# Single-pass matrix products that read their columns from two halves in turn, in a two-layer encoder kernel

## The chip, the cores and the metric

The kernel runs on one core of one Trainium2 chip. The metric is the device time of one execution in microseconds (us), the median of the runs. Kernels that are compared ran on the same chip.

## The reference

The model has two layers on 512 frames of width 1024 and 256 memory tokens. Everything is float32. Layer 0 mixes time with a gated recurrence (12 heads of 64), layer 1 with chunked attention; both also attend to the memory, project the result back and add a gated feed-forward block with a short convolution:

```python
p = rms_norm(x, ln1) @ w_in               # 1024 -> mixer columns | memory queries
mix = rwkv7_time_mix(...)                 # layer 0;  chunk_attention(...) in layer 1
mo = memory_attention(q_mem, mem_n, w_mem_kv[layer])
x = x + jnp.concatenate([mix, mo], -1) @ w_out[layer]
gate, val = jnp.split(rms_norm(x, ln2) @ ffn_in, 2, -1)      # 1024 -> 2 x 2816
conv = conv_b + sum(conv_w[j] * shifted(gate, 2 - j) for j in range(3))
x = x + (gelu(conv, approximate=False) * val) @ ffn_out      # 2816 -> 1024
```

## The kernel before

Activations lie with features on the 128 partitions and the 512 frames along the free dimension. Every large product is done in two parts of float32r ("single-pass" here, against plain float32): a tile is split into a high part (a rounded copy, by ScalarE) and a low part (the rest, by VectorE, or by a DMA that adds into it), and three matmuls per tile of the contraction, high x high, high x low and low x high, are summed in PSUM. A matmul has a stationary operand of 128 columns, loaded ahead of it (PEld in the profile), and a moving operand whose columns are streamed through the array.

The places that the change and the prediction's steps touch:

- `dense` (L233 to L248) makes one 128 x 512 product from 8 tiles of the contraction with 24 matmuls. The weights `whi`, `wlo` are stationary and the 512 frames of the activations (`r1h`, `r1l`, `r2h`, `r2l`) move. It serves the projections of both mixers, `out_proj` (L396) and, with 256 memory tokens, `mem_kv` (L1040).
- `ffn` (L415 to L929) has three parts. First the `mixer` generator prepares operands while `out_proj` runs. Then come 21 frames per layer, one for each 128 of the 2816 hidden columns (the last tile goes through `dense`). A frame (`Seven.frame`, L537) makes gate and value with seven products in place of eight, each of 128 x 256 columns from 4 tiles, by `prod` (L427): 12 matmuls, 84 for the frame. Their results stand in the PSUM tiles `f1` to `f4`, read by one ScalarE copy (L553) and five VectorE sums (L509, L572, L585, L601, L603). Inside a frame the instructions of VectorE and ScalarE are pinned in the order in which they are written (`keep`). VectorE also makes the sums of weights for the next frame and the low parts (L486, L491, L495, L504, L481); three DMAs of POOL's queue add into tiles (`wlv` L471, `wlo` L477, `tmp` L522). Every second frame (`APART`) leaves half of one low part to such a DMA.
- Last, `out_by_seven` (L763) projects back. There the hidden activations are stationary and the weights move, 512 columns at a time (`rows`, L692 to L703), again with seven products for eight (L749 and after).
- `v_proj` (L1754) and the values of `mem_kv` (L1055 to L1062) also have the weights as moving operand, 256 columns at a time. The scores of the attention (L1788, L1789) and the score of the memory attention move 128 to 512 columns of keys; transposes, small products of the recurrence and the products with the attention weights (L370, L1817) are in plain float32.

The program is one straight list per engine, and the order is set when it is built: by the order in which the code is written, by `weave` (L87), which interleaves generators by estimated costs, and by a scheduler that keeps dependencies.

Of the kernel before, what the change touches and what calls it, by code (L numbers as in the profile page):

```python
# [12 lines left out]
AF = mybir.ActivationFunctionType  # L13
# [46 lines left out]
def _constants():  # L60
    f = np.float32
    c = np.zeros((P, NCST), f)

    def put(name, a):
        o, n = COFF[name]
        c[:, o:o + n] = a

    i = np.arange(P)
    same = (i[:, None] // 64) == (i[None, :] // 64)
    put("ident", np.eye(P, dtype=f))  # L70
    put("ones_d", np.full((P, 2), 1.0 / 1024, f))
# [12 lines left out]
    return c  # L84

# [36 lines left out]
def trunk_kernel(ctx, tc, A, out):  # L122
# [97 lines left out]
    def mm3(ps, wh, wl, ah, al, start, stop):  # L220
        PE.matmul(ps, wh, ah, start=start, stop=False)
        PE.matmul(ps, wh, al, start=False, stop=False)
        PE.matmul(ps, wl, ah, start=False, stop=stop)
# [8 lines left out]

    def dense(ps, units, act, order=None, start=True, stop=True):  # L233

        ks = [(w, j, k) for w, kk in units for j, k in enumerate(kk)]
        if order is not None:
            ks = [next(q for q in ks if q[2] == k) for k in order]

        for n, ((wh, wl), j, k) in enumerate(ks):
            ah, al = act(k)  # L240
            PE.matmul(ps, wh[:, j * P:(j + 1) * P], ah, start=start and n == 0, stop=False)  # L241
            dense_at[0] = PE.matmul(ps, wh[:, j * P:(j + 1) * P], al, start=False, stop=False)  # L242
            yield 432
        for n, ((wh, wl), j, k) in enumerate(ks):
            dense_at[0] = PE.matmul(ps, wl[:, j * P:(j + 1) * P], act(k)[0], start=False,  # L245
                                    stop=stop and n == len(ks) - 1)
            if n % 2 or n == len(ks) - 1:
                yield 432 if n % 2 else 216  # L248
# [149 lines left out]
    def out_proj(l, act, taken, xT, order, pre=(), done=()):  # L398
        for m in range(KD):
            if m < len(pre):  # L400
                w, ps = pre[m]
                run(dense(ps[:], [(w, K8)], act, order=[k for k in order if k not in done], start=False))
            else:
                w = load_w(A["w_out"][l, m])
                ps = ps_f() if m in (2, 3) else ps_d()
                run(dense(ps[:], [(w, K8)], act, order=order))
            V.tensor_tensor(xT[:, m], xT[:, m], ps[:], op=ALU.add)
            next(taken)
# [8 lines left out]
    def ffn(l, hp, U, T, new_x, xT, after=None, tokens=None):  # L417
# [7 lines left out]
        XU = lambda o, h: [tuple(t[:, 2 * k + o, h * 256:h * 256 + 256] for t in (Uh, Ul)) for k in range(4)]  # L425
        XT = lambda i: [tuple(t[:, 2 * k + i // 2, i % 2 * 256:i % 2 * 256 + 256] for t in (Th, Tl)) for k in range(4)]
# [20 lines left out]
        class Seven:  # L447
# [59 lines left out]
            def end1(self):  # L507
                g, f4 = self.g, self.f4
                keep(V.tensor_tensor(g[:], g[:], f4[:], op=ALU.add))  # L509
# [24 lines left out]
            def end5(self):  # L534
                keep(V.tensor_tensor(hid32[self.j], self.v[:], self.c[:], op=ALU.mult))

            def frame(self, prev2, prev, nxt, norm=None, ending=None):  # L537
# [15 lines left out]
                keep(SC.copy(g[:, h1], f1[:, h1]))  # L553
# [18 lines left out]
                keep(V.tensor_tensor(g[:, h2], g[:, h1], f2[:, h1], op=ALU.subtract))  # L572
# [12 lines left out]
                keep(V.tensor_tensor(c[:, h1], f1[:, h2], g[:, h2], op=ALU.subtract))  # L585
# [11 lines left out]
                if first:  # L597
# [3 lines left out]
                keep(V.tensor_tensor(v[:].rearrange("p (a s) -> p a s", a=2), c[:, h1].unsqueeze(1).to_broadcast([P, 2, 256]),  # L601
                                     f3[:].rearrange("p (a s) -> p a s", a=2), op=ALU.add))
                keep(V.tensor_tensor(g[:, h2], g[:, h2], f3[:, h2], op=ALU.subtract))  # L603
# [11 lines left out]
        def ending():  # L615
# [30 lines left out]
            keep(V.tensor_tensor(g[:], pg[:], rho[:], op=ALU.mult))  # L646
            run(dense(pv[:], [(wv[:2], KO)], pair_of(Uh, Ul)))
            tile21 = Seven(j)
            tile21.g, tile21.c, tile21.v = g, c, pv
# [42 lines left out]
        def rows(pss, act, k0, ch, first, last):  # L692
            hi, lo, n = ch
            for t, ps in pss:
                ts = slice(t * P, t * P + P)
                for i in range(n):
                    for a in act:
                        PE.matmul(ps[:], a[:, k0 + i, ts], hi[:, i * S:i * S + S],  # L698
                                  start=bool(first) and (first is True or t in first) and a is act[0] and i == 0, stop=False)
            for t, ps in pss:  # L700
                ts = slice(t * P, t * P + P)
                for i in range(n):
                    PE.matmul(ps[:], act[0][:, k0 + i, ts], lo[:, i * S:i * S + S], start=False, stop=bool(last) and t in last and i == n - 1)  # L703
# [311 lines left out]
    def lora_pair(idx, w, wm):  # L1015
# [6 lines left out]
        V.tensor_tensor(b_[:], pb[:], rho[:], op=ALU.mult)  # L1022
        z = tmp()
        V.tensor_tensor(z[:], pa[:], rho[:], op=ALU.mult)
# [14 lines left out]
    def mem_kv():  # L1039
# [3 lines left out]
        for l in range(2):  # L1043
            km, vm_ = (kmT0, vm0) if l == 0 else (tmp(F32, (P, 2, 256)) for _ in range(2))
            for f in range(2):
                w = load_w(A["w_memk"][l, f])
                ps = ps_l()
                yield from dense(ps[:, :NMEM], [(w, K8)], pair_of(mh, ml))
                yield from norm
                V.tensor_tensor(km[:, f], ps[:, :NMEM], macc[:, NMEM:], op=ALU.mult)  # L1050
            ps = [ps_l(), ps_l()]
            for u in range(2):
                wh, wl = load_w(A["w_memv"][l, u])
                for j in range(4):
                    k = u * 4 + j  # L1055
                    for t in range(2):
                        ws = slice(j * 256, (j + 1) * 256)
                        ts = slice(t * P, (t + 1) * P)
                        pt = ps[t][:, :256]
                        PE.matmul(pt, mh[:, k, ts], wh[:, ws], start=k == 0, stop=False)  # L1060
                        PE.matmul(pt, ml[:, k, ts], wh[:, ws], start=False, stop=False)
                        PE.matmul(pt, mh[:, k, ts], wl[:, ws], start=False, stop=k == 7)  # L1062
                    yield 650
# [35 lines left out]
    def head_wide(src, fix, bank, tied=False):  # L1099
# [5 lines left out]
        with behind_dense() if tied else ExitStack():  # L1105
            PE.matmul(ps[:], blk1[:], hi[:], start=True, stop=False)
            PE.matmul(ps[:], blk1[:], lo[:], start=False, stop=True)
        a, y, sh = tmp(), tmp(), tmp()
        fix(a[:], ps[:])
# [16 lines left out]
    def prepare(i, T):  # L1126
# [13 lines left out]
        PE.matmul(pz[:], wah[:, 0], zw[:], start=True, stop=False)  # L1140
        PE.matmul(pa[:], wah[:, 1], zs[:], start=True, stop=False)
        PE.matmul(pz[:], wal[:, 0], zw[:], start=False, stop=True)
        PE.matmul(pa[:], wal[:, 1], zs[:], start=False, stop=True)
# [3 lines left out]
        SC.activation(sig[:], pz[:], AF.Tanh, scale=0.5, bias=aw0h[:, 6 + i:7 + i])  # L1147
        V.tensor_scalar(sig[:], sig[:], 0.5, 0.5, op0=ALU.mult, op1=ALU.add)
        th = kt_("a")
        SC.activation(th[:], pa[:], AF.Tanh, scale=0.5, bias=aw0h[:, i:i + 1])  # L1150

        def proj(j, nm, nxt):
# [7 lines left out]
            V.tensor_tensor(p_[:], ps[:], rho[:], op=ALU.mult)  # L1160
# [99 lines left out]
        def bonus():  # L1260
# [8 lines left out]
            PE.matmul(pb[:], blk1[:], rkh[:], start=True, stop=False)  # L1269
            PE.matmul(pb[:], blk1[:], rkl[:], start=False, stop=True)  # L1270
# [14 lines left out]
        V.tensor_tensor(bon[:], T["pb"][:], T["v"][:], op=ALU.mult)  # L1285
# [218 lines left out]
    def dst_mix(i, yc, pg):  # L1504
        V.tensor_tensor(yc[:], yc[:], pg[:], op=ALU.mult)
# [5 lines left out]
    def q_mem(src, act, qm):  # L1511
        for f in range(2):
# [3 lines left out]
            V.scalar_tensor_tensor(qm[f], ps[:], 0.125, rho[:], op0=ALU.mult, op1=ALU.mult)  # L1516
# [169 lines left out]
    with ExitStack() as bctx:  # L1686
# [38 lines left out]
        def q_split(ps, T):  # L1725
            q = tmp()
            V.scalar_tensor_tensor(q[:], ps[:], 0.125, rho[:], op0=ALU.mult, op1=ALU.mult)
# [7 lines left out]
        def k_proj(i, T, ps=None):  # L1735
# [6 lines left out]
            V.tensor_tensor(k_[:], ps[:], rho[:], op=ALU.mult)  # L1742
# [11 lines left out]
        def v_proj(g, wv=None):  # L1754
# [3 lines left out]
            for t2 in range(2):  # L1758

                pp_ = ps_d() if g else ps_s()  # L1760
                for t in (2 * t2, 2 * t2 + 1):
                    pt = pp_[:, (t % 2) * 256:(t % 2) * 256 + 256]
                    ts = slice(t * P, (t + 1) * P)
                    for k in range(8):
                        wh, wl = wv[k // 4]
                        ws = slice((k % 4) * 256, (k % 4 + 1) * 256)
                        PE.matmul(pt, r1h[:, k, ts], wh[:, ws], start=k == 0, stop=False)
                        PE.matmul(pt, r1l[:, k, ts], wh[:, ws], start=False, stop=False)
                        PE.matmul(pt, r1h[:, k, ts], wl[:, ws], start=False, stop=k == 7)
# [191 lines left out]

def layout(i):
# [26 lines left out]
    A["w_memv"] = np.stack([_vtile(g["w_mem_kv"][l][:, 256:])[0] for l in range(2)])  # L1989
# [13 lines left out]
    A["ffn_out7"] = np.stack(seven)  # L2003
    A["ffn_outp"] = np.stack(plain)
    A["lnf"] = np.ascontiguousarray(np.broadcast_to(g["ln_f"][None, :], (P, KD * P)))
    A["w_kvk"] = _wtile(g["w_kv"][:, :768])
    A["w_kvv"] = _vtile(g["w_kv"][:, 768:])
# [24 lines left out]
```

## Time and profile before

| | |
|---|---|
| runs | 1291.62, 1293.07, 1292.89 us, median 1292.89 |
| span of the profiled execution | 1292.6 us (0.3 us under the median of the runs) |
| mean granted TensorE clock | 0.997 |
| busy: PE, PEld, DVE, ACT, POOL | 98%, 84%, 80%, 65%, 12% |
| DMA | 192.14 MB moved, mean 149 GB/s |

The profile is of one execution. PE rows are matmuls; they are pipelined, so that one begins before the one ahead of it ends, and the step from start to start is what a matmul costs in a stream. A group `psf<-th,whi` writes the PSUM tile `psf` from `th` and `whi`; `128*128 128x256` is the stationary shape, then the output. Idle time is told with what ended it. A window row gives, for a stretch of time, each engine's busy us and number of instructions, the granted clock, the DMA engines' busy share and GB/s.

### The profile page before, as it was taken

To read this page: it belongs to the slowest core of one execution; us is meant where nothing else is said; L and a number is where in the kernel's file an instruction comes from. 1 tells how busy PE (TensorE), PEld (TensorE's weight loads), DVE (VectorE), ACT (ScalarE), POOL (GpSimd) and SP (SyncE) were. 2 spreads that over 40 slices of the span, in tenths; PEclk is the share of its full clock that TensorE was granted. 3 is DMA by queue.
4 is the path that set the end of the run, shared out by engine and by line. 5 is a ranking of instruction groups with operands and counts; after the bars stand their busy time and mean duration, and the time that the engine had idled before them with its cause. 6 is when DMAs were issued, how large, how long until landed. Compare 5 with 4: busy or idle time off the path is not lost.

```text
span 1292.6 us, 26432 instructions
## 1 busy us (share of the span) xinstructions
PE 1260.9 (98%) x10420; PEld 1083.1 (84%) x10420; DVE 1031.7 (80%) x1956; ACT 846.4 (65%) x1398; POOL 152.7 (12%) x182
## 2 busy tenths in 40 slices
PE   9999999999999999999999999999999999999997
PEld 7887777777789999998888878787789999998886
DVE  7867677765688999998876876658889999998684
ACT  6566767856476777776554676757757777765662
POOL 1000000000001222320220000000002222211200
PEclk9999999999999999999999999999999999999999
DMA  5364444453055988996984322234429989978951
GB/s 204 110 174 106 100 96 89 92 109 96 30 166 126 212 198 198 206 208 172 274 185 122 118 87 82 76 104 123 130 61 212 197 193 211 208 161 262 233 149 66
DMA packets 95581, 192.14 MB, mean 149 GB/s; under 512 B 22112, under 2 KB 30432, under 8 KB 95456
## 3 DMA queue, kind: packets, MB, share of 16 engines
q1 hardware_dynamic: 68592, 129.14, 31.9%
q0 software_dynamic: 26864, 61.31, 27.3%
q8 instruction: 82, 1.34, 0.4%
q14 instruction: 43, 0.35, 0.1%
HBM read 174.20 MB, written 6.29 MB: 140 GB/s over the span
## 4 chain that ended last, share of the span: by engine, by line
PE 62%; DVE 15%; ACT 8%; DMA 8%; issue 6%; SPq 0%; POOL 0%; ACTq 0%; DVEq 0%; POOLq 0%
PE psf L434 8%; PE psf L698 7%; PE psd L245 6%; PE psd L241 5%; PE psd L242 5%; DMA wlv<-in_ffn_in_dram 4%; PE psf L436 4%; PE psf L703 4%; PE psd L698 3%; ACT whi L499 2%; DMA wraw<-in_ffn_in_dram 2%; PE psd L703 2%; DVE raw L486 1%; PE pss L1817 1%; DVE wlo L504 1%
## 5 line engine op out<-in xcount | busy, mean ns | idle before, releaser
L499 ACT CAST whi<-raw 128x1024 fp32r<-128x1024 f32 (+1 forms) x168 | 153.3, 942 | 62.3 <-PE psf L434 29.5
L434 PE MATMUL psf<-th,whi 128*128 128x256 f32 x672 | 161.4, 278 | 2.5 <-ACT tmp L553 1.9
L434 PE MATMUL psf<-tl,whi 128*128 128x256 f32 x672 | 161.1, 276 | 0.0
L195 ACT CAST whi<-wraw 128x1024 fp32r<-128x1024 f32 x84 | 87.6, 1048 | 78.3 <-PE psd L242 37.4
L434 PEld LDWEIGHTS psf<-th,whi 128*128 128x128 f32 x672 | 125.8, 188 | 3.9 <-ACT tmp L553 2.9
L434 PEld LDWEIGHTS psf<-tl,whi 128*128 128x128 f32 x672 | 126.0, 188 | 0.0
L504 DVE TENSOR_TENSOR wlo<-raw,whi 128x1024 fp32r<-128x1024 f32 (+1 forms) x108 | 109.3, 1012 | 9.1 <-ACT whi L499 8.9
L241 PE MATMUL psd<-r1h,whi 128*128 128x512 f32 x264 | 107.4, 408 | 0.0
L242 PE MATMUL psd<-r1l,whi 128*128 128x512 f32 x264 | 105.0, 398 | 0.0
L203 DVE TENSOR_TENSOR wlo<-wraw,whi 128x1024 fp32r<-128x1024 f32 x65 | 79.2, 1219 | 22.3 <-ACT whi L195 20.4
L688 ACT CAST whi<-raw 128x1024 fp32r<-128x1024 f32 (+1 forms) x52 | 49.6, 954 | 59.9 <-PE psf L698 33.1
L689 DVE TENSOR_TENSOR wlo<-raw,whi 128x1024 fp32r<-128x1024 f32 (+1 forms) x52 | 56.5, 1097 | 38.9 <-ACT whi L688 31.5
L436 PE MATMUL psf<-th,wlo 128*128 128x256 f32 x504 | 78.0, 276 | 0.0
L245 PE MATMUL psd<-r1h,wlo 128*128 128x512 f32 x264 | 74.3, 403 | 0.6 <-DMA wlo<-in_ffn_in_dram 0.4
L471 POOL DMA_DIRECT2D wlv<-in_ffn_in_dram x40 | 60.7, 1516 | 59.5 <-DVE tmp L572 59.1
L436 PEld LDWEIGHTS psf<-th,wlo 128*128 128x128 f32 x504 | 66.8, 188 | 0.0
L434 PE MATMUL psf<-r2h,whi 128*128 128x256 f32 x252 | 60.9, 278 | 0.7 <-ACT whi L499 0.7
L434 PE MATMUL psf<-r1h,whi 128*128 128x256 f32 x252 | 60.7, 277 | 0.7 <-ACT whi L499 0.7
L434 PE MATMUL psf<-r2l,whi 128*128 128x256 f32 x252 | 60.7, 277 | 0.0
L434 PE MATMUL psf<-r1l,whi 128*128 128x256 f32 x252 | 60.6, 277 | 0.0
L241 PEld LDWEIGHTS psd<-r1h,whi 128*128 128x128 f32 x264 | 49.6, 188 | 12.0 <-issue 2.1
L525 ACT ACTIVATE tmp<-tmp,vec 128x512 f32<-128x512 f32 x44 | 36.0, 817 | 33.3 <-DVE tmp L512 33.3
(611 smaller groups left out, 3576.8 us busy)
## 6 DMA issues: line engine op xcount, KB each, us to landing
raw<-in_ffn_in_dram SPq DMA_DIRECT2D x42, 512.0 KB, 5.2
raw<-in_ffn_in_dram SPq DMA_DIRECT2D x84, 256.0 KB, 5.5
wlv<-in_ffn_in_dram POOLq DMA_DIRECT2D x40, 512.0 KB, 8.6
raw<-in_ffn_out_dram SPq DMA_DIRECT2D x30, 512.0 KB, 6.2
raw<-in_ffn_out_dram POOLq DMA_DIRECT2D x24, 512.0 KB, 8.4
wraw<-in_wA_dram SPq DMA_DIRECT2D x20, 512.0 KB, 4.1
wraw<-in_w_out_dram SPq DMA_DIRECT2D x16, 512.0 KB, 4.1
wraw<-in_ffn_outp_dram SPq DMA_DIRECT2D x16, 512.0 KB, 4.5
```

Source lines behind the costliest of these rows:

```text
L195: high = lambda: pin(SC.copy(hi[:, :n], raw))
L203: pin(V.tensor_tensor(lo[:, :n], raw, hi[:, :n], op=ALU.subtract))
L241: PE.matmul(ps, wh[:, j * P:(j + 1) * P], ah, start=start and n == 0, stop=False)
L242: dense_at[0] = PE.matmul(ps, wh[:, j * P:(j + 1) * P], al, start=False, stop=False)
L245: dense_at[0] = PE.matmul(ps, wl[:, j * P:(j + 1) * P], act(k)[0], start=False, stop=stop and n == len(ks) - 1)
L434: PE.matmul(ps, wh[:, o + k * P:o + k * P + P], x[k][n], start=k == n == 0, stop=False)
L436: PE.matmul(ps, wl[:, ol + k * P:ol + k * P + P], x[k][0], start=False, stop=k == 3)
L471: GP.dma_start(self.low[:].rearrange("p (a s) -> p a s", a=2), self.second, accum_op=ALU.add)
L499: keep(SC.copy(hi[:, :n], self.pair(what) if n > S else self.raw[:, what]))
L504: keep(V.tensor_tensor(lo[:, :n], self.pair(what) if n > S else self.raw[:, what], hi[:, :n], op=ALU.subtract))
L698: PE.matmul(ps[:], a[:, k0 + i, ts], hi[:, i * S:i * S + S], start=bool(first) and (first is True or t in first) and a is act[0] and i == ...
L703: PE.matmul(ps[:], act[0][:, k0 + i, ts], lo[:, i * S:i * S + S], start=False, stop=bool(last) and t in last and i == n - 1)
```

## The change

Wherever a product in float32r has 512 or 256 columns, its moving operand is now read through a view that takes one column from the first half of the range, one from the second half, the next of the first, and so on (`woven`). The matmul writes its output without gaps, so the columns stand in PSUM in that mixed order. Whoever reads them out reads one half of the columns with a step of 2 from PSUM and then the other half with a step of 2 (`plain_order`), and writes the two halves one behind the other (`halved` splits the SBUF side into the same shape). Where the weights move (`rows`, `v_proj`, the values of `mem_kv`) the host stores the weights in the opposite order (`_woven`), so that the output comes out in plain order and the readers stay as they were. Plain float32 products, transposes and the scores of the attention are as before. The diff, cut to its core:

```diff
+def woven(t):
+    return t.rearrange("p (a b) -> p b a", a=2)
+def halved(t):
+    return t.rearrange("p (a b) -> p a b", a=2)
+def plain_order(ps):
+    return ps.rearrange("p (b a) -> p a b", a=2)
...
+    def moving(hl):
+        return [woven(t) for t in hl]
...
     def dense(ps, units, act, order=None, start=True, stop=True):
-            ah, al = act(k)
+            ah, al = moving(act(k))
...
-        XU = lambda o, h: [tuple(t[:, 2 * k + o, h * 256:h * 256 + 256] for t in (Uh, Ul)) for k in range(4)]
+        XU = lambda o, h: [tuple(woven(t[:, 2 * k + o, h * 256:h * 256 + 256]) for t in (Uh, Ul)) for k in range(4)]
...
-                keep(SC.copy(g[:, h1], f1[:, h1]))
+                keep(SC.copy(halved(g[:, h1]), plain_order(f1[:, h1])))
...
-                keep(V.tensor_tensor(g[:, h2], g[:, h1], f2[:, h1], op=ALU.subtract))
+                keep(V.tensor_tensor(halved(g[:, h2]), halved(g[:, h1]), plain_order(f2[:, h1]), op=ALU.subtract))
...
-                        PE.matmul(ps[:], a[:, k0 + i, ts], hi[:, i * S:i * S + S],
+                        PE.matmul(ps[:], a[:, k0 + i, ts], woven(hi[:, i * S:i * S + S]),
...
-            V.tensor_tensor(p_[:], ps[:], rho[:], op=ALU.mult)
+            V.tensor_tensor(halved(p_[:]), plain_order(ps[:]), halved(rho[:]), op=ALU.mult)
...
+def _woven(w, n=S):
+    return np.ascontiguousarray(w.reshape(*w.shape[:-1], -1, n // 2, 2).swapaxes(-1, -2)).reshape(w.shape)
...
-    A["ffn_out7"] = np.stack(seven)
+    A["ffn_out7"] = _woven(np.stack(seven))
```

The readers that got the step are those of `out_proj` (L407), of the frames (L509, L553, L572, L585, L601, L603) and of the last hidden tile (L646, L535), and those of the projections (L1022, L1024, L1050, L1109, L1147, L1150, L1160, L1285, L1505, L1516, L1727, L1742).

No instruction is added, removed or moved: on every engine the same operations stand in the same order. Only some of PE's waits differ: 191 rows of its list wait for an earlier matmul's own count (PE_49) where 165 did. Most of the added ones are in the frames whose first low part VectorE makes. This is PE's list before, at the second product of such a frame (`th`, `tl` are the summed activations, `r2h` a high part, `whi` and `wlo` the weights):

```order
L436 MATMUL psf<-r2h,wlo 128x256 [waits DVE_49]
L436 MATMUL psf<-r2h,wlo 128x256 x3
L434 MATMUL psf<-th,whi 128x256
L434 MATMUL psf<-tl,whi 128x256
L434 MATMUL psf<-th,whi 128x256
```

And this is PE's list at the same place now:

```order
L452 MATMUL psf<-r2h,wlo 128x256 [waits DVE_49]
L452 MATMUL psf<-r2h,wlo 128x256 x3
L450 MATMUL psf<-th,whi 128x256 [waits PE_49]
L450 MATMUL psf<-tl,whi 128x256
L450 MATMUL psf<-th,whi 128x256
```

The matmuls are the same; the first of the second product has got a wait for a matmul that stands ahead of it on the same engine.

More of the change, by code (lines that the diff above doesn't have):

```diff
@@ L220, in mm3 @@
     def mm3(ps, wh, wl, ah, al, start, stop):
+        ah, al = woven(ah), woven(al)
         PE.matmul(ps, wh, ah, start=start, stop=False)
@@ L244, in dense @@
         for n, ((wh, wl), j, k) in enumerate(ks):
-            dense_at[0] = PE.matmul(ps, wl[:, j * P:(j + 1) * P], act(k)[0], start=False,
+            dense_at[0] = PE.matmul(ps, wl[:, j * P:(j + 1) * P], moving(act(k))[0], start=False,
                                     stop=stop and n == len(ks) - 1)
@@ L702, in rows @@
                 for i in range(n):
-                    PE.matmul(ps[:], act[0][:, k0 + i, ts], lo[:, i * S:i * S + S], start=False, stop=bool(last) and t in last and i == n - 1)
+                    PE.matmul(ps[:], act[0][:, k0 + i, ts], woven(lo[:, i * S:i * S + S]), start=False, stop=bool(last) and t in last and i == n - 1)
         def seventh(pss, raw, act, first=True, last=True, read=None, side=()):
@@ L1268, in bonus @@
             pb = ps_s()
-            PE.matmul(pb[:], blk1[:], rkh[:], start=True, stop=False)
-            PE.matmul(pb[:], blk1[:], rkl[:], start=False, stop=True)
+            PE.matmul(pb[:], blk1[:], woven(rkh[:]), start=True, stop=False)
+            PE.matmul(pb[:], blk1[:], woven(rkl[:]), start=False, stop=True)
             T["pb"] = pb
@@ L1766, in v_proj @@
                         ws = slice((k % 4) * 256, (k % 4 + 1) * 256)
[L1767 to L1769 removed]
+                        PE.matmul(pt, r1h[:, k, ts], woven(wh[:, ws]), start=k == 0, stop=False)
+                        PE.matmul(pt, r1l[:, k, ts], woven(wh[:, ws]), start=False, stop=False)
+                        PE.matmul(pt, r1h[:, k, ts], woven(wl[:, ws]), start=False, stop=k == 7)
                         yield 324
```

68 lines of the change are left out of this document (35 added, 33 removed).

## The prediction

> **What bounds the kernel now.** I read the page first: its span, busy times and chain of waits.
>
> ```profile
> span 1292.6 us, 26432 instructions
> PE 1260.9 (98%) x10420; PEld 1083.1 (84%) x10420; DVE 1031.7 (80%) x1956; ACT 846.4 (65%) x1398; POOL 152.7 (12%) x182
> PE 62%; DVE 15%; ACT 8%; DMA 8%; issue 6%; SPq 0%; POOL 0%; ACTq 0%; DVEq 0%; POOLq 0%
> ```
>
> PE is busy nearly throughout and holds 62% of the chain. The shares differ by stage, so next the windows: the frames of layer 0 and of layer 1, the two stretches in which the hidden activations are projected back, the first mixer, the first `out_proj`, and the second mixer with the end of layer 0's projection.
>
> ```profile
> 395.45:590.02 194.57, 192.07 (x1667) 190.29 (x1667) 185.55 (x287) 140.74 (x189) 49.70 (x48) 1.00 0.87 194
> 953.98:1150.95 196.97, 191.96 (x1670) 190.36 (x1670) 186.14 (x287) 142.31 (x189) 49.65 (x48) 1.00 0.87 192
> 600.00:690.00 90.00, 89.30 (x396) 73.28 (x396) 72.13 (x74) 51.50 (x62) 13.88 (x16) 1.00 0.86 227
> 1161.00:1292.60 131.60, 123.67 (x558) 101.31 (x556) 95.08 (x124) 65.61 (x88) 13.87 (x16) 0.99 0.65 180
> 0.00:345.00 345.00, 334.18 (x4321) 259.92 (x4322) 248.82 (x674) 227.07 (x448) 18.33 (x36) 1.00 0.44 110
> 345.00:390.00 45.00, 45.00 (x204) 35.98 (x203) 33.79 (x54) 26.84 (x38) 1.75 (x2) 1.00 0.45 141
> 690.00:950.00 260.00, 255.99 (x1389) 204.66 (x1388) 185.97 (x427) 168.78 (x358) 3.75 (x14) 1.00 0.31 97
> ```
>
> PE is busy for 94% or more of each. Beside it VectorE (the third pair) is busy 95% in the frames, about 80% in the projections back and 72% in the mixers; the DMA engines reach 0.86 or 0.87 in the frames and the first projection back. So PE sets the time almost everywhere, and in the frames VectorE is close behind. The granted clock is full throughout. What one matmul costs PE is its step from start to start, which the timeline gives, here of 512-column, then of 256-column products:
>
> ```profile
> 600.27 0.39 PE L241 MATMUL psd<-r2h,whi 128*128 128x512 f32 x1
> ...
> 601.40 0.39 PE L242 MATMUL psd<-r2l,whi 128*128 128x512 f32 x1
> 1001.48 0.28 PE L434 MATMUL psf<-r1h,whi 128*128 128x256 f32 x1
> ...
> 1002.39 0.28 PE L436 MATMUL psf<-r1h,wlo 128*128 128x256 f32 x1
> ```
>
> Five steps take 1.13 us, 0.226 each; eight take 0.91, 0.114 each. That is 0.442 and 0.444 ns a column: the cost grows with the columns and leaves no room for a fixed part. Products in plain float32 read the same kind of tile:
>
> ```profile
> 334.83 0.59 PE L370 MATMUL pss<-E,vm 128*64 128x512 f32 x1
> 335.25 0.59 PE L370 MATMUL pss<-KB,vm 128*64 128x512 f32 x1
> ```
>
> Each takes 0.42 us for 512 columns. It goes over them at about half the pace, and half of 0.42 is 0.21, not 0.226. So the array can step faster than the single-pass products let it; about 7% of their time by these rounded rows goes with the columns that pass at the full pace. Reading the moving operand is the obvious suspect, and its order is what the change alters.
>
> **Products of 512 columns.** How many there are by stage: the windows of the weights' high parts, which two of each three matmuls use.
>
> ```profile
> 0.00:345.00 345.00, 131.72 (x521) 88.23 (x521) 21.77 (x18) 36.99 (x37) 1.00 0.44 110
> 345.00:390.00 45.00, 30.28 (x129) 23.27 (x127) 7.30 (x6) 7.13 (x7) 1.00 0.45 141
> 600.00:690.00 90.00, 62.94 (x256) 47.72 (x256) 34.13 (x31) 30.00 (x31) 1.00 0.86 227
> 690.00:950.00 260.00, 151.12 (x630) 108.13 (x630) 40.47 (x34) 35.59 (x34) 1.00 0.31 97
> 1161.00:1292.60 131.60, 83.11 (x336) 62.08 (x334) 39.20 (x35) 34.23 (x35) 0.99 0.65 180
> ```
>
> Less the 256-column ones that the code puts there (128 and 192), times 1.5: 590, 194, 384, 657 and 504, together 2329. The price of a woven read does not stand in this trace. From below, at full pace it cannot be under 0.205 us, half of 0.42 with its rounding, a gain of 21 ns; from above it is unbounded, since each read could pay for a change of place (a rival). I take 0.215, half of 0.42 rounded up, since the rows nearest to it pass as many columns: a gain of about 12 ns. That is 7.1, 2.3, 4.6, 7.9 and 6.0 us. The second and third stages hardly have idle PE, and I keep 2.3 and 4.2, the latter for the crowded DMA engines. The mixers hold serial chains of small products, where a faster `dense` only arrives early: I keep three quarters, 5.3 and 5.9. The last stage ends with idle PE, 5.5. Sum 23 us.
>
> The Trainium skill (TensorE: Matmul & The Clock Gate, Back-to-back issue gap) gives for an isolated warm matmul columns / 2.4 + 2.5 ns, 216 ns for 512; the trace does not agree, with 226. By it the gain would be at most about 10 ns a product, 19 us in place of 23.
>
> **Frames.** A frame has 84 matmuls, 84 x 0.1135 = 9.53 us, yet the 20 frames of the first window take 194.57 / 20 = 9.73 us and the second's 9.85. Two things cap what faster reads give. First the weights: a product of only two columns still follows the one ahead of it by
>
> ```profile
> 24.13 0.47 PE L311 MATMUL pss<-cst,acc 128*128 128x2 f32 x3
> L311 PE MATMUL pss<-cst,acc x32: 165/251/272, 23.7 to 954.2; 128*128 128x2 f32 x32
> ```
>
> (0.47 - 0.25) / 2 = 0.11 us, since each loads 128 columns of weights. A 256-column product at 0.1135 can come down to that, not below: up to 3.5 ns, 0.29 us a frame, 12 us for all 42. Second VectorE, whose instructions stand in one pinned row from one low part to the next frame's:
>
> ```profile
> 1110.95 1.22 DVE L504 TENSOR_TENSOR wlo<-raw,whi 128x1024 fp32r<-128x1024 f32 x1
> ...
> 1118.25 1.23 DVE L504 TENSOR_TENSOR wlo<-raw,whi 128x1024 fp32r<-128x1024 f32 x1 [0.31 <-ACT whi L499]
> ...
> 1120.92 1.22 DVE L504 TENSOR_TENSOR wlo<-raw,whi 128x1024 fp32r<-128x1024 f32 x1
> ```
>
> Such a frame takes it 9.97 us with 0.31 idle; the frame between has a shorter low part. So VectorE has hardly any room, and a faster PE will wait for its low parts, or for the late `wlv`:
>
> ```profile
> PE psf L436 <- DMA wlv<-in_ffn_in_dram: 4.1, 7, 1.6
> ```
>
> I take 4 us of the 12, ends 0 and 12. The other 480 products of 256 columns give 1 us. Total 23 + 4 + 1 = 28.
>
> **Readers.** Five sums on VectorE read PSUM in each frame:
>
> ```profile
> L601 DVE TENSOR_TENSOR tmp<-tmp,psf 128x512 f32<-128x512 f32 x42 | 28.6, 680 | 0.2
> L509 DVE TENSOR_TENSOR tmp<-tmp,psf 128x512 f32<-128x512 f32 x42 | 28.5, 679 | 0.0
> L585 DVE TENSOR_TENSOR tmp<-psf,tmp 128x256 f32<-128x256 f32 x42 | 17.5, 417 | 0.2
> L603 DVE TENSOR_TENSOR tmp<-tmp,psf 128x256 f32<-128x256 f32 x42 | 17.4, 413 | 0.0
> L572 DVE TENSOR_TENSOR tmp<-tmp,psf 128x256 f32<-128x256 f32 x42 | 17.4, 413 | 0.0
> ```
>
> That is 2 x 512 + 3 x 256 = 1792 columns. No row reads PSUM with a step of 2. The nearest read SBUF, L1233 with a step of 16 columns on its inputs and L1235 in runs of 15, both 120 columns:
>
> ```profile
> L1233 DVE TENSOR_TENSOR Xu<-Lr,cst x6: 351/356/360, 77.9 to 283.3; 128x120 f32<-128x120 f32 x6
> L1235 DVE TENSOR_TENSOR Xsa<-cst,Xu x3: 273/278/283, 78.8 to 243.4; 128x120 f32<-128x120 f32 x3
> ```
>
> So a far step costs up to 78 / 120 = 0.65 ns a column. A step of 2 is much nearer to runs than to 16, and I take 0, with 0.65 as the other end; I see no way to a gain. ScalarE, 72% busy in the frames, has room for one such copy. Elsewhere the step lies on engines with a fifth or more of their time free. The woven weights change only the order of bytes in memory, the same DMAs bring them: 0.
>
> **Waits.** The 26 added waits of PE on itself name matmuls already in its stream. Behind each stand the rest of the frame's matmuls, and VectorE and ScalarE wait for these. Each frame has one such wait already, at its fourth product:
>
> ```profile
> 1005.24 0.63 PE L436 MATMUL psf<-th,wlo 128*128 128x256 f32 x4
> 1005.70 0.28 PE L434 MATMUL psf<-th,whi 128*128 128x256 f32 x1
> ```
>
> Four matmuls in 0.46 us, then the waiting one with no gap: 0. If a wait did drain PE, 0.28 us x 26 would be 7 us, the other end.
>
> **The rivals.** *No effect*: the extra 7% belongs to single-pass arithmetic or to the writing of PSUM, and not to the order of reading. Against it speaks that a cost in step with the columns fits a stream of reads; for it, that no row here reads in another order. Then 1293 us.
>
> *The readers eat it* (slower): at 0.65 ns a column a frame gets 1.16 us on VectorE, which has no room, 42 x 1.16 = 49 us, and the frames' own 4 us are lost: 1292.9 + 49 - 24 = 1318 us. It decides from 24 / 42 = 0.57 us a frame on, 0.32 ns a column. For it speaks VectorE's 95%; against it that 2 is a small step.
>
> *Each read pays* (slower, far): every column of a woven read lies elsewhere than the last, and if PE pays for each, a single-pass product falls to the pace of the plain ones, 0.42 for 512 and 0.21 for 256. That is 2329 x 0.194 + 4010 x 0.0965 = 839 us, so some 2130. It decides from an average of about 12 ns in 512 columns on. For it speaks that streams which do not change place run so near to full pace; against it that a plain product's half pace shows reading with time to spare. The Trainium skill (SBUF — State Buffer, Specifications) speaks for it: lines of 16 bytes, at least two hits in each for full bandwidth, and a penalty for each crossing. A woven read has one hit before it leaves a line, though it returns to it. By it today's reads, four floats to a line, pay nothing. No run here shows that rule.
>
> **How the numbers follow.** The forecast, faster reads, 0.61: 1292.6 - 28 = 1264.6, and 0.3 for the median of the runs, 1265 us. It spans 1243 (21 ns on each 512-column product at the kept three quarters, 37 us, plus the frames' 12 us and 1) to 1288. No effect 0.12, 1293. Readers 0.12, 1318. Each read 0.13, 2130. In 0.02 the new order meets the weights' reads badly and costs a little. The range 1243 to 1318 leaves out the far rival and some edges, 0.18. A measurement of this kernel tells 0.2%, 2.6 us, from no change: faster 0.61, same 0.12, slower 0.27.
>
> **What would show it.** Right: steps of about 0.215 us in L241's and 0.11 in L434's successors, VectorE's five sums at 680 and 415 ns as now, frames near 9.6 us that wait for VectorE. Wrong: steps of 0.226 and 0.1135 as before (no effect); sums of 800 ns or more (readers); steps of 0.25 or more (each read pays).

## The result and the profile after

The changed kernel takes 1270.43 us (median of 4 runs, 1269.46 to 1272.55), the one before 1292.82 beside it (1291.62 to 1293.07). The ratio is 0.9834, 95% interval 0.982 to 0.9848: 22.4 us less between the medians. The profiled execution after is one of 1269.46 us, the shortest of its four, and its span is 24.9 us shorter than the one before. Page of the changed kernel: span, the line of busy times for PE, the chain by engine.

```profile
span 1267.7 us, 26431 instructions
PE 1224.1 (97%) x10420; PEld 1074.6 (85%) x10420; DVE 1030.5 (81%) x1956; ACT 842.0 (66%) x1398; POOL 152.9 (12%) x182
PE 53%; DVE 18%; DMA 11%; ACT 9%; issue 8%; POOL 0%; SPq 0%; ACTq 0%; DVEq 0%; POOLq 0%
```

PE is busy 36.8 us less with as many matmuls; the other engines work as long as before. PE's share of the chain fell from 62% to 53%, those of VectorE and DMA rose: part of the gain met other waits. Timeline of PE, first products of 512 columns, then of 256 in a frame:

```profile
592.00 0.38 PE L257 MATMUL psd<-r2h,whi 128*128 128x512 f32 x1
...
593.73 0.38 PE L257 MATMUL psd<-r2h,whi 128*128 128x512 f32 x1
...
990.23 0.28 PE L450 MATMUL psf<-th,whi 128*128 128x256 f32 x1
...
991.12 0.61 PE L452 MATMUL psf<-th,wlv 128*128 128x256 f32 x4
```

Eight products lie between the first two rows, 1.73 / 8 = 0.216 us each (0.226 before), and eight between the last two, 0.89 / 8 = 0.111 (0.1135 before). In the trace's own records, which are in nanoseconds, the commonest step of 512 columns went from 227 to 216, that of a frame's 256 from 113 to 112; the means without waits (steps under 245 and under 125 ns) went from 228.1 to 215.8 and from 113.8 to 111.7. Groups on VectorE, the readers of PSUM in steps of 2:

```profile
L619 DVE TENSOR_TENSOR tmp<-tmp,psf 128x512 f32<-128x512 f32 x42 | 28.6, 681 | 0.2
L603 DVE TENSOR_TENSOR tmp<-psf,tmp 128x256 f32<-128x256 f32 x42 | 17.5, 417 | 0.2
L590 DVE TENSOR_TENSOR tmp<-tmp,psf 128x256 f32<-128x256 f32 x42 | 17.4, 413 | 0.0
```

They take 681, 417 and 413 ns where they took 680, 417 and 413. Where the time went, by stage: windows cut at the same instructions in both (first product of the first frame, last of the frames, first and last of the output rows, and so on). Columns as on the page: length, then busy time and count of each engine. The kernel before:

```profile
0.00:387.60 387.60, 376.78 (x4508) 293.77 (x4509) 281.44 (x727) 253.91 (x486) 20.07 (x38) 1.00 0.45 114
387.60:597.40 209.80, 206.64 (x1780) 204.08 (x1780) 196.81 (x304) 150.03 (x201) 50.61 (x49) 1.00 0.83 184
610.20:723.30 113.10, 113.10 (x514) 93.59 (x513) 86.50 (x96) 65.39 (x87) 13.88 (x16) 1.00 0.70 183
723.30:949.30 226.00, 221.99 (x1227) 176.49 (x1226) 162.49 (x395) 151.24 (x331) 3.75 (x14) 1.00 0.32 101
949.30:1158.30 209.00, 203.92 (x1772) 202.10 (x1771) 196.43 (x303) 152.26 (x201) 50.56 (x49) 1.00 0.84 185
1171.10:1284.70 113.60, 113.60 (x518) 93.95 (x517) 84.52 (x104) 60.75 (x82) 13.87 (x16) 1.00 0.68 183
```

And the changed kernel:

```profile
0.00:379.90 379.90, 364.65 (x4508) 291.97 (x4509) 279.51 (x724) 252.68 (x486) 20.08 (x38) 1.00 0.45 117
379.90:590.10 210.20, 204.11 (x1780) 200.79 (x1779) 197.87 (x305) 149.09 (x202) 50.63 (x49) 1.00 0.82 184
602.90:711.10 108.20, 107.68 (x513) 94.11 (x512) 86.22 (x96) 65.83 (x88) 13.89 (x16) 1.00 0.73 192
711.10:932.40 221.30, 214.44 (x1228) 174.90 (x1227) 162.63 (x396) 150.43 (x330) 3.85 (x14) 1.00 0.32 103
932.40:1138.60 206.20, 201.53 (x1772) 198.99 (x1771) 195.34 (x302) 149.39 (x201) 50.55 (x49) 1.00 0.84 187
1151.80:1259.80 108.00, 108.00 (x518) 94.51 (x517) 84.09 (x105) 60.11 (x82) 13.87 (x16) 1.00 0.71 192
```

The four stages of 512-column products became shorter by 7.7, 4.9, 4.7 and 5.6 us, 22.9 together. The first stretch of frames became 0.4 longer, the second 2.8 shorter. The pieces in between became 0.4 longer: 22.9 + 2.4 - 0.4 = 24.9. In the mixers part of the gain became idle time: in the first row PE's busy time fell by 12.1 us, the stage by 7.7.

A part of the 7.7 is not the change's. In the profiled execution before, the granted clock was halved for 3.4 us of the first stage, and the one after has no such stretch there:

```profile
49.80:53.20 3.40, 3.40 (x18) 3.40 (x17) 3.30 (x24) 2.11 (x3) 0.00 (x0) 0.50 0.35 136
```

In the records 15 products of 256 columns step there by 213 or 214 ns, where those behind them take about 118: some 1.5 us, an estimate. That it all reached the end of the stage isn't shown, but the sizes fit. The times of runs lie 1.7 to 1.9 us above their spans wherever both are on record, so the profiled execution before took about 1294.3 us (an estimate), 1.5 above its median, and the one after was 1.0 below its own: 24.9 - 1.5 - 1.0 = 22.4.

In the frames most of the gain was lost. Twenty of them, from first to last ScalarE copy, after:

```profile
389.13:582.87 193.74, 189.51 (x1667) 187.21 (x1667) 184.83 (x285) 139.90 (x189) 49.72 (x48) 1.00 0.86 196
937.03:1131.36 194.33, 189.77 (x1670) 187.48 (x1670) 185.42 (x286) 140.32 (x188) 49.64 (x48) 1.00 0.87 194
```

Before they took 194.57 and 196.97. An undisturbed frame is 84 x 111.7 ns = 9.38 us now (84 x 113.3 = 9.52 before), but the mean is 9.70 (before 9.79). Over both sets the products by these steps cost 375.3 us instead of 380.7, 5.4 less, and all else in these 40 frames 12.8 instead of 10.8. So in this pair 2.0 of the 5.4 came back as waits. Each is one execution: in the three kernels below with the same woven frames and other output rows, both sets together took 387.3 to 389.1 us (here 388.1 after and 391.5 before), so the pair alone doesn't settle these 2 us.

### The profile page after: what moved, and what is told of

Read it like the earlier page. It is cut to its first block, busy times and chain, and to the rows that moved or that the text cites. A ratio compares the mean times of both kernels' runs of the same rounds, so it can differ in the third digit from the quotient of the medians.

```text
span 1267.7 us, 26431 instructions
## 1 busy us (share of the span) xinstructions
PE 1224.1 (97%) x10420; PEld 1074.6 (85%) x10420; DVE 1030.5 (81%) x1956; ACT 842.0 (66%) x1398; POOL 152.9 (12%) x182
## 4 chain that ended last, share of the span: by engine, by line
PE 53%; DVE 18%; DMA 11%; ACT 9%; issue 8%; POOL 0%; SPq 0%; ACTq 0%; DVEq 0%; POOLq 0%
PE psf L450 7%; PE psf L716 7%; DMA wlv<-in_ffn_in_dram 6%; PE psd L261 4%; PE psf L452 4%; PE psf L721 3%; PE psd L257 3%; PE psd L258 3%; PE psd L716 3%; DVE wlo L215 2%; DMA wraw<-in_ffn_in_dram 2%; PE psd L721 1%; PE pss L1835 1%; ACT whi L515 1%; PE pss L716 1%
## 5 line engine op out<-in xcount | busy, mean ns | idle before, releaser
L515 ACT CAST whi<-raw 128x1024 fp32r<-128x1024 f32 (+1 forms) x168 | 150.7, 939 | 52.5 <-DVE raw L507 24.1
L450 PEld LDWEIGHTS psf<-th,whi 128*128 128x128 f32 x672 | 128.7, 192 | 3.7 <-ACT tmp L571 2.8
L450 PEld LDWEIGHTS psf<-tl,whi 128*128 128x128 f32 x672 | 128.8, 192 | 0.0
L257 PE MATMUL psd<-r1h,whi 128*128 128x512 f32 x264 | 104.0, 395 | 0.0
L258 PE MATMUL psd<-r1l,whi 128*128 128x512 f32 x264 | 101.6, 386 | 0.0
L706 ACT CAST whi<-raw 128x1024 fp32r<-128x1024 f32 (+1 forms) x52 | 49.4, 949 | 50.5 <-PE psf L716 27.3
L261 PE MATMUL psd<-r1h,wlo 128*128 128x512 f32 x264 | 70.6, 390 | 2.5 <-DVE wlo L215 1.4
```

Source lines behind the costliest of these rows:

```text
L261: dense_at[0] = PE.matmul(ps, wl[:, j * P:(j + 1) * P], moving(act(k))[0], start=False, stop=stop and n == len(ks) - 1)
L450: PE.matmul(ps, wh[:, o + k * P:o + k * P + P], x[k][n], start=k == n == 0, stop=False)
L515: keep(SC.copy(hi[:, :n], self.pair(what) if n > S else self.raw[:, what]))
```

## The experiments

**Which products.** Two kernels split the change. The first is the changed kernel with the frames plain again:

```
-        XU = lambda o, h: [tuple(woven(t[:, 2 * k + o, ...]) for t in (Uh, Ul)) ...]
+        XU = lambda o, h: [tuple(t[:, 2 * k + o, ...] for t in (Uh, Ul)) ...]
-                keep(SC.copy(halved(g[:, h1]), plain_order(f1[:, h1])))
+                keep(SC.copy(g[:, h1], f1[:, h1]))
```

(and so XT and the frames' other five readers), so the 512-column products and the other 256-column ones stay woven, "the wide products" from here on; the second has these edits reversed, in the kernel before.

> The changed kernel with the frames' 256-column products and the frames' readers put back as before; the 512-column products and the other 256-column ones stay woven. Theory A (the gain is nearly all in the 512-column products, and frames gain only what their step loses): about 1271 to 1275 us, 18 to 22 us under the kernel before; the frames' product step is back at 0.113 us and the 512-column step stays at 0.215. Rival B (a good part, over 6 us, comes from the frames): 1279 us or more. If the frames' weaving gave nothing, 1270.

> The kernel before with only the frames' 256-column products read from two halves in turn and the frames' readers of PSUM in steps of 2. Theory A: 1 to 5 us under the kernel before (1288 to 1292): 840 columns' steps a frame set fall from 0.113 to 0.112, and the readers cost what they did (681 and 413 ns). Rival B: 6 us or more under it (below 1287). Rival C, readers in steps of 2 cost something that other gains hid: above 1293.

The wide products alone: 1271.47 us (5 runs), ratio 0.9849 (0.9834 to 0.9865), against 0.9834 for all. The frames alone: 1291.07 (12 runs), ratio 0.9997 (0.9988 to 1.0007). Theory A holds: nearly all the gain is the wide products', and what the frames add is within the uncertainty. Yet the edit works there too. Timeline of PE with the frames alone woven:

```profile
500.01 0.28 PE L446 MATMUL psf<-r2h,whi 128*128 128x256 f32 x1
...
500.90 0.61 PE L448 MATMUL psf<-r2h,wlv 128*128 128x256 f32 x4
```

0.89 / 8 = 0.111, the fast step. The sets of 20 frames with the wide products alone woven:

```profile
388.27:582.17 193.90, 191.51 (x1667) 189.99 (x1667) 185.17 (x286) 140.92 (x188) 49.70 (x48) 1.00 0.88 194
937.70:1132.70 195.00, 191.84 (x1670) 190.14 (x1670) 185.88 (x287) 143.41 (x189) 49.65 (x48) 1.00 0.89 194
```

193.90 and 195.00 with the plain step, 193.74 and 194.33 with the woven one: 0.8 us less over both sets, where the products cost 5.4 less. The mean frame hardly gets shorter with its products.

**What holds the frames.** Three runs on it. First the late weights: the POOL queue's DMA that adds onto `wlv` is left out.

```
-                GP.dma_start(self.low[:].rearrange("p (a s) -> p a s", a=2), self.second, accum_op=ALU.add)
```

> The changed kernel without the DMA that adds the second weights' low part onto the first: the addition of that low part is left out. Theory (the frames that last 9.8 to 11.3 us instead of 9.4 wait for this DMA, which the profile names): 4 to 8 us less than the changed kernel, 1262 to 1266. Rival (the wait is there but another one, high weights or VectorE, ends just behind it): 1268 to 1271.

1269.18 us (1268.31 to 1271.28), ratio 0.9818 (0.9799 to 0.9837). That lies in the rival's range: about 1 us under the changed kernel, which the intervals don't tell from none. PE's waits in the frames, changed kernel:

```profile
PE psf L452 <- DMA wlv<-in_ffn_in_dram: 4.6, 7, 1.3
PE psf L450 <- ACT tmp L571: 2.0, 3, 1.1
PE psf L450 <- ACT whi L515: 1.6, 2, 0.8
```

Without that DMA the first row is gone, the DMA share in the first set falls from 0.86 to 0.57, and the set still takes 193.5 us; this row stands first now:

```profile
PE psf L450 <- ACT whi L514: 2.4, 4, 0.8
```

Then VectorE: one of its operations per frame left out, in the changed kernel and in the one with only the wide products woven.

```
-                keep(V.tensor_tensor(halved(g[:, h2]), halved(g[:, h2]), plain_order(f3[:, h2]), op=ALU.subtract))
```

> The changed kernel without one VectorE operation of 0.41 us in each of the 43 times it stands in the frames: it leaves out the subtraction of one product from the second half of the gate's sum. VectorE is busy 95% of the frames' time and the products 98%, so each may be what holds the mean frame at 9.7 us. Theory (VectorE's work and what follows it set the mean frame; the woven products' step no longer shows): frames of 9.4 us nearly throughout, 8 to 12 us less than the changed kernel, 1258 to 1262. Rival (the products and their waits for weights set it): 1267 to 1271.

> The kernel with only the wide products woven, without the same VectorE operation (it leaves out the same subtraction). Theory (with VectorE's work shorter, the step of the frames' products is what is left, 9.52 us a frame instead of 9.38): 4 to 6 us longer than the changed kernel without that operation. Rival (the frames' step never shows): within 1.5 us of it.

It stands 42 times, 17.4 us of VectorE. The time fell to 1266.01 us (1262.89 to 1267.33), ratio 0.9795 (0.9775 to 0.9815); with plain frames to 1268.05 (1265.26 to 1270.61), 0.9813 (0.9788 to 0.9838). Less than the theory's 8 to 12 us, a little more than the rival allows. The first set, with the operation left out of the changed kernel:

```profile
388.42:579.72 191.30, 188.10 (x1667) 186.58 (x1667) 179.93 (x267) 142.59 (x188) 49.70 (x48) 1.00 0.89 198
```

VectorE is busy for 4.9 us less there, and the set takes 2.4 less. The other set (194.20) takes 0.1 less, but the granted clock was halved for 3.4 us in it, with 15 products at 213 ns, which is worth about 1.5 us (an estimate). So VectorE's work does hold back part of the frames, and no single supplier holds them all: without the DMA other waits took its place, and without part of VectorE's work the wait for `wlv` still stands first (5.7 us over both layers). The 2.0 us between the two kernels, what the frames' weaving might be worth with VectorE eased, lies inside their spread and is not settled.

**Which order of reading.** The weights can be laid out for any order, so the changed kernel was run with others for four groups of products. The edit in each is of this kind, with the host's layout to match:

```
-    PE.matmul(ps[:], a[:, k0 + i, ts], woven(hi[:, i * S:i * S + S]), ...)
+    PE.matmul(ps[:], a[:, k0 + i, ts], hi[:, i * S:i * S + S].rearrange("p (a b) -> p b a", a=4), ...)
```

> The changed kernel, with other reading orders where the operand is a weight that can be laid out to suit: the plain output rows read columns 2 apart (256 groups in turn), the seventh ones from four quarters in turn, the output values of the projection in runs of 4 columns (16 bytes) from each half, the memory's values 16 columns (64 bytes) on at each read. Theory 1 (a step lost for each new 64 bytes of one stream; a second stream hides it): quarters 0.215 to 0.216 per 512 columns, runs of 4 0.112 per 256, 2 apart about 0.240, 64 bytes on at each read much slower, up to twice the time. Theory 2 (consecutive reads of the same 64 bytes are what costs): quarters 0.216, 64 bytes on at each read 0.112, 2 apart 0.227. Theory 3 (any pattern of two dimensions is read faster than a plain one): all at 0.216 and 0.112. Theory 4 (each 16-byte line that is left costs a step): quarters no better than halves, runs of 4 the best, 2 apart clearly the fastest.

> As the run with quarters, with other orders: the plain output rows read 64 bytes (16 columns) on at each read (32 groups in turn), the seventh ones in runs of 16 columns (64 bytes) from each half, the output values of the projection from 8 groups in turn (32 columns, 128 bytes apart), the memory's values 4 columns (16 bytes) on at each read. Theory 1 (a step lost for each new 64 bytes of one stream): 64 bytes on at each read much slower, up to 0.43 per 512 columns; runs of 16 about 0.227; 8 groups 0.112; 16 bytes on at each read 0.13 per 256 columns. Theory 2 (consecutive reads of the same 64 bytes cost): 64 bytes on 0.216, runs of 16 0.227, 16 bytes on 0.113. Theory 3 (any pattern of two dimensions is fast): all at 0.216 and 0.112.

They took 1409.1 and 1401.6 us (one run each). Timeline of PE in the first of these kernels, seventh rows and then plain ones:

```profile
645.14 1.30 PE L736 MATMUL psd<-wlo,r2h 128*128 128x512 f32 x4
646.28 1.30 PE L728 MATMUL psd<-whi,r2h 128*128 128x512 f32 x4
...
730.43 0.63 PE L726 MATMUL psf<-whi,th 128*128 128x512 f32 x1
...
732.24 0.63 PE L726 MATMUL psf<-whi,th 128*128 128x512 f32 x1
```

From quarters in turn a product takes 1.14 / 4 = 0.285 us, from columns 2 apart 1.81 / 4 = 0.453. And in the second kernel, runs of 16 (seventh rows), 64 bytes on at each read (plain rows), and 8 groups (the projection's output values):

```profile
645.96 1.12 PE L736 MATMUL psd<-wlo,r2h 128*128 128x512 f32 x4
646.91 1.36 PE L728 MATMUL psd<-whi,r2h 128*128 128x512 f32 x5
...
721.01 0.61 PE L726 MATMUL psf<-whi,th 128*128 128x512 f32 x1
...
722.31 0.61 PE L726 MATMUL psf<-whi,tl 128*128 128x512 f32 x1
...
849.35 0.40 PE L1801 MATMUL psd<-whi,r1l 128*128 128x256 f32 x1
849.57 0.40 PE L1802 MATMUL psd<-wlo,r1h 128*128 128x256 f32 x1
```

0.95 / 4 = 0.238, 1.30 / 3 = 0.433, and 0.22 for 256 columns. All four theories fall: theory 1 got the 64-byte steps right, but had quarters, 8 groups and runs of 4 as fast and 2 apart at 0.240; theory 2 had quarters and 64 bytes on as fast; theory 3 has every order fast; theory 4 had 2 apart as the fastest, and it is the slowest. A second set of theories went into one more kernel, in which all orders take two columns in turn.

> The changed kernel with four more reading orders that all take two columns in turn, from the weights laid out to suit. Plain output rows: in groups of 4 columns the order 0, 2, 1, 3. Seventh output rows: two runs of 16 columns (64 bytes apart) in turn, then the next 32 columns. Memory's values: two runs of 32 columns in turn. Output values of the projection: columns 0, 128, 2, 130 and so on, then 1, 129, 3, 131 and so on. Theory 5, formed after the runs with other orders (columns are fetched in pairs of 8 bytes, and a pair's second column is free only if it is read at most two reads later): the three orders in blocks at 0.215 to 0.22 per 512 columns and 0.112 per 256, the skipping one at about 0.220 per 256, since no pair's second column is read soon. Theory 6 (a pattern whose innermost count is 2 is read fast wherever it points): all four at 0.216 and 0.112. Theory 7 (it matters that the two streams lie far apart): 0, 2, 1, 3 and the runs of 16 at 0.227 or more.

1273.8 us (one run). Its timeline, the seventh rows (runs of 16 in turn) and the plain ones (0, 2, 1, 3):

```profile
620.21 1.03 PE L736 MATMUL psd<-wlo,r2h 128*128 128x512 f32 x4
621.07 1.24 PE L728 MATMUL psd<-whi,r2h 128*128 128x512 f32 x5
...
681.75 0.39 PE L726 MATMUL psf<-whi,tl 128*128 128x512 f32 x1
...
682.65 0.39 PE L726 MATMUL psf<-whi,tl 128*128 128x512 f32 x1
```

0.86 / 4 = 0.215, as fast as the halves with only 64 bytes between the streams; 0.90 / 4 = 0.225, as slow as the plain order. All orders together, the median step in the records (for the plain order by stage; the orders of the three kernels with other layouts are from one execution each):

| order of reading | columns | ns |
|---|---|---|
| plain, in mixers and output rows | 512 | 227 to 231 |
| two halves in turn | 512 / 256 | 216 / 112 |
| two runs of 16 in turn; two of 32 | 512; 256 | 216; 112 |
| 0, 2, 1, 3 in groups of 4 | 512 | 227 |
| 0, 128, 2, 130, ... | 256 | 118 |
| 4 columns of each half | 256 | 127 |
| 16 columns of each half | 512 | 240 |
| four quarters in turn | 512 | 283 |
| 8 groups; 16 groups in turn | 256 | 220; 220 |
| 32 groups in turn (64 bytes on) | 512 | 433 |
| 4 columns on at each read | 256 | 233 |
| 2 columns on at each read | 512 | 451 |

Theory 5 fails on the skipping order (118, not 220) and on 0, 2, 1, 3; theory 6 on the same two, which it had at 112 and 216; theory 7 on the runs of 16. What holds in all runs is narrower: of the orders tried, two streams at least 64 bytes apart, each read without a gap, one column of each in turn, run at the fast step; one stream pays 11 ns in 512 columns, and four streams or more cost from 31% to about double. In all of them the matmul writes PSUM in the same way and does the same arithmetic, so it is the order of reading that sets the step. What the reader does inside stays open.

**Where the operands lie.** The kernel shifts low weights and narrow tiles in SBUF by 32 and 16 columns. Both kernels without that:

```
-W_AT = {"whi": 0, "wlo": 32}
-W_NARROW = 16
+W_AT = {"whi": 0, "wlo": 0}
+W_NARROW = 0
```

> The kernel before with the two gaps taken out that shift the weights' low parts and narrow tiles against the others in SBUF (32 and 16 columns become 0). If the time of a step hung on where the two operands lie against each other, steps go up: 512-column products from 0.227 to over 0.230, 256-column ones from 0.113 towards 0.118 or more, the kernel 3 to 30 us longer. If the gaps do nothing now: 1293.

> The changed kernel with the same two gaps taken out. Theory: reading from two halves in turn also takes away what a step owed to the place of its operands, so the steps stay at 0.215 and 0.112 and the time at 1270. Rival: the place matters as before, and the time goes up by what the kernel before without the gaps goes up.

The kernel before rose to 1305.23 us (ratio to itself with the gaps 1.009, 1.0068 to 1.0112), the changed one stood at 1272.02 (1271.4 to 1278.54; ratio to the kernel before with the gaps 0.9849, 0.982 to 0.9878). Timeline of a frame's products in the kernel before without the gaps:

```profile
500.04 0.28 PE L434 MATMUL psf<-r2h,whi 128*128 128x256 f32 x1
...
501.00 0.64 PE L436 MATMUL psf<-r2h,wlv 128*128 128x256 f32 x4
```

And in the changed one without them:

```profile
500.46 0.28 PE L450 MATMUL psf<-th,whi 128*128 128x256 f32 x1
...
501.35 0.61 PE L452 MATMUL psf<-th,wlo 128*128 128x256 f32 x4
```

0.96 / 8 = 0.120 without the weave, 0.89 / 8 = 0.111 with it. So a plain read also pays for where its operand lies, up to 7 ns in 256 columns, and the woven one doesn't: the theory holds. Longer products do show in the frames: without the gaps the two sets of the kernel before took 200.20 and 199.90 us, 8.6 more together.

**What bounds 256 columns.** Two kernels cut all but the first of a quarter's twelve products, to 128 and to 32 columns:

```
-    PE.matmul(ps, wl[:, ol + k * P:ol + k * P + P], x[k][0], start=False, stop=k == 3)
+    PE.matmul(ps[:, 0:P], wl[:, ol + k * P:ol + k * P + P], x[k][0][:, 0:64], start=False, stop=k == 3)
```

(This is the edit for 128; for 32 it has `0:32` and `0:16`.)

> The changed kernel, with all but the first of the twelve products of a frame's quarter cut to 128 columns: it leaves out half of these products' columns. Theory (a 256-column step is now bounded by the load of the next weights): the step of the cut products stays at 0.10 to 0.112 us though they have half the columns, and the kernel changes by less than 10 us. Rival (256 columns are bounded by their own reading, and the weights' load is shorter): steps fall to about 0.06 us, and the frames become bound by VectorE, 7 to 8 us a frame instead of 9.4.

> The changed kernel, with all but the first of the twelve products of a frame's quarter cut to 32 columns: it leaves out most of these products' columns. At 128 columns a product took four times its columns (0.213 us), so 32 columns would be 0.053 us by their own reading. Theory (a 256-column step is bounded by the load of the next weights): the cut products' step stays at 0.10 to 0.112 us and the kernel within 15 us of the changed one. Rival (bounded by reading): 0.053 to 0.06 us, and the frames last as long as VectorE's work, 7 to 9.4 us.

Both were far slower, 1611.9 and 1608.7 us (one run each), which neither theory had. The page's row of PE's clock, in 40 slices, for 32 columns:

```profile
PEclk9999999998555555555999999997555555555999
```

A window of the frames with 32 columns:

```profile
400.00:580.00 180.00, 180.00 (x846) 180.00 (x846) 98.81 (x144) 72.82 (x96) 25.74 (x25) 0.50 0.51 114
```

The granted clock was 0.50 through nearly all of the frames. The timeline there, and then in the first 4 us of layer 1's frames, in which the clock was still full:

```profile
502.41 0.37 PE L453 MATMUL psf<-tl,whi 128*128 128x32 f32 x1
...
503.26 0.37 PE L453 MATMUL psf<-tl,whi 128*128 128x32 f32 x1
...
1103.30 0.26 PE L453 MATMUL psf<-r1h,whi 128*128 128x32 f32 x1
...
1103.97 0.60 PE L455 MATMUL psf<-r1h,wlo 128*128 128x32 f32 x4
```

At the halved clock the step is 0.85 / 4 = 0.21 us (213 ns in the records) for 32 columns, and the same for 128, so the columns don't set it, and the "four times its columns" of the second expectation misread the halved clock. At full clock it is 0.67 / 6 = 0.112, and in the kernel with 128 columns too (111 or 112 ns in the records of both). So at full clock products of 2, 32 and 128 columns and the woven ones of 256 all step by 111 to 112 ns: a woven read of 256 columns stands on a floor that doesn't depend on its columns, as the theory has it, and a still faster read of 256 columns would give nothing. That the floor is the load of the next weights is likely, as all these products load 128 columns of them, but no run changes that load.

## Why the prediction was right, point by point

- **PE sets the time, and reading is the suspect.** Right. The array's own pace, read off the plain float32 products, was 0.21 us for 512 columns, and the woven step came to 0.216. The Trainium skill (TensorE: Matmul & The Clock Gate, Back-to-back issue gap) gives 216 ns for an isolated warm matmul of 512 columns; the trace agrees for the woven read, and not for the plain one, with 227.
- **512 columns: 12 ns each, 23 us kept.** The 12 ns were right (11 for the commonest step, 12.3 in the mean), and the stages gave 22.9 us; that this met 23 is in part luck. The first two stages were put at 5.3 + 2.3 and gave 7.7, but about 1.5 of that is the halved clock of the profile before; the projection back 4.2 and 4.9, the second mixer 5.9 and 4.7, the last rows 5.5 and 5.6. So the three quarters kept in the mixers were too much in both, by some 1.4 and 1.2 us, and the rows gave 0.8 more than was put.
- **Frames: 4 us of 12.** 2.4 in the profiled pair, and nothing that the measurement tells in the split kernels. The cap from the weights' load was right in size (0.11): products of 32 columns come down to 0.112 and not below. That late `wlv` and a VectorE without room would take the rest was right in kind; no single one of them does. This term was too large, and so was the 1 us for the other products, of which no sign is left once the stages' 22.9 are counted.
- **Readers: 0.** Right, to 1 ns. The rival that priced a step of 2 by a far step in SBUF (0.65 ns a column) didn't occur, nor did the one without effect, by which the order of reading would not matter.
- **Waits: 0.** Right: the 40 steps from a first product's last matmul (`r2h,wlo` or `r1h,wlo`) to the `th,whi` behind it, where most of the added waits stand, are all 111 or 112 ns.
- **Each read pays: 2130 us.** It did not happen with two streams, but the price was real: with 32 groups in turn a product takes 0.433 us where the rival had 0.42. Its mistake was the point from which it decides, more than two streams and not one change of place. The Trainium skill (SBUF — State Buffer, Specifications) has a penalty for each crossing of a 16-byte line; the halves leave the line at each read and are the fastest order measured, so for two streams the measurement decides against it, and from four quarters on the runs show a cost of that kind.

The forecast was 28 us; the medians differ by 22.4, the profiled pair by 24.9, or about 23.4 without the halved clock. The mechanism was right; what the mixers, the frames and the small products would keep of it was sized about 5 us too large together.

## What to carry to other kernels

When products come back to back, divide their step by the columns and compare it with another kind of product on the same array: a surplus in step with the columns may lie in the reading, as it did here, and then a layout can remove it. Two runs read in turn, 64 bytes apart or more, took 5% off the step of 512 columns; four or more made it 31% longer and up, so try the order on one group of products before laying out a kernel for it. Products that already stand on the floor of narrow ones (here 112 ns) have nothing to gain. Where a stage is held by several suppliers at once, count only what the product and its slowest neighbours both allow.

## What the runs showed beside it

- A plain read's step depends on where operands lie in SBUF (113 to 120 ns in the frames when two gaps were removed); the woven read's does not (112 in both). The gaps that the kernel before needed are no longer needed, as far as these runs tell (1272.02 without them, 1270.43 with).
- Reading PSUM in steps of 2 costs VectorE nothing (681 against 680 ns for 512 columns).
- With narrow products the granted clock fell to 0.50 in the frames, 4 and 9 us after they began, and stayed there although the profile has PE busy in all of the 180 us shown. What makes it fall stays open. The Trainium skill (TensorE: Matmul & The Clock Gate, Part 1: The HAM clock gate) tells of a gate that halves the clock when PE is idle; the trace agrees on the half, but shows it without idle time on PE.
